# Gate and up with x stationary over 512 columns, twelve of 22 column blocks by seven half-products, down chunk by chunk

## The chip, the cores and the metric

The kernel runs on one core of a Trainium2 chip. The metric is the device time of one execution in microseconds, and the comparison is made on the median of several runs. A profile is one further execution, recorded by the hardware profiler; its span runs from the first to the last instruction, and its own device time is given beside it. Engines are named as the profile names them: PE (matrix unit; PEld is its weight load), DVE (vector), ACT (scalar), POOL (GpSimd) and SP (issues the DMAs).

## The reference

A trunk of two layers over x of 256 tokens by 1024 channels, float32. Each layer is a SwiGLU block, a mixer and a second SwiGLU block, every one behind an RMS norm and added to x:

```python
for layer in range(DEPTH):                     # DEPTH = 2, SEQ = 256, D_MODEL = 1024, D_FF = 2816
    x = x + 0.5 * _swiglu(_rmsnorm(x, ffn1_norm[layer]), gate, up, down)
    h = _rmsnorm(x, mix_norm[layer])
    x = x + (_even_mixer(h, ...) if layer % 2 == 0 else _pool_mixer(h, ...))
    x = x + 0.5 * _swiglu(_rmsnorm(x, ffn2_norm[layer]), gate, up, down)

def _swiglu(h, w_gate, w_up, w_down):
    return (jax.nn.silu(h @ w_gate) * (h @ w_up)) @ w_down
```

So there are four SwiGLU blocks, each with two products of 256x1024 by 1024x2816 and one of 256x2816 by 2816x1024. The even mixer has an input projection of 2560 columns, a spatial gate, attention over eight heads with a mask, and an output projection. The odd mixer multiplies four channel groups by 256x256 matrices and takes centred averages over the tokens.

## The kernel before

**Arithmetic.** Every large product is made in three passes over float32r operands: each operand a is split into a high part (a rounded by ACT when it writes float32r) and a low part (a minus the high part, on DVE), and high·high, high·low and low·high are accumulated in PSUM. `mm3` (L283) has the weights stationary, 128 by 128, and x moving, 256 tokens wide. `mm3x` (L289) has 128 tokens of x stationary and the weights moving; the even mixer's `natural` (L356) uses it over 512 columns.

**Weights.** All weights lie in DRAM as chunks of 16 blocks of 128 by 128 (1 MB), in the order of use: for a SwiGLU block 22 chunks of gate and up, one for each block of 128 columns of the hidden width, then 11 of down. `Weights` (L46) streams them: `load` (L63) issues one DMA of 1 MB into one of three `raw` tiles, `split_hi` (L79) makes `wh` by an ACT copy of 512 columns, `split_lo` (L89) makes `wl` by a DVE subtraction of 512 columns. Sixteen pairs of split tiles let the split run up to 15 steps of four blocks ahead of PE. `take` (L124) hands the next blocks to PE; at every fourth block `boundary` (L118) runs the small tasks that the code has put at that step with `at`, and then `pump` (L102) one or two splits. The order of each engine's queue is the order in which this code emits its instructions.

**A SwiGLU block** (`ffn`, L296). For each of 22 column blocks, gate and up are accumulated over the eight slices of the 1024 channels into two PSUM banks, hidden columns on the partitions and tokens along the row. `finish` (L302) puts three tasks at later steps: DVE multiplies by the row of norm factors and ACT takes the silu; DVE multiplies by up and ACT writes `yh`; DVE writes `yl`. All of y, 22 blocks high and low, is kept. After the last column block, down runs output block by output block (eight of them, 22 blocks of y each), and DVE scales the result by half the norm factor and adds it to X (L347, L348). `Norm` (L220) holds the next norm: x times gain, split high and low (L228, L231), the squares and their sum (L240, L242), and from it the factors: `columns` (L248) sums over partitions on PE, raises to the power −1/2 on POOL (L271) and refines on DVE; `rows` (L257) spreads them along the tokens by another PE product.

**Even mixer** (`even_mixer`, L366): `natural` for keys, queries, gate values and attention values, `prepare` (L419) for the norm and the rotary turn of queries and keys, `spatial`, `pair` for two heads, then the output projection into four banks and the update of X.

**Odd mixer** (`odd_mixer`, L602): four groups with x stationary, with `columns` emitted after the second of them; ACT and DVE copy the four banks scaled by the norm factors (L618, L619), then eight pairs of products with the averaging matrices (L626, L627) and the update of X (L628).

**Start.** x comes in four DMAs of 256 KB, the first chunk of weights in four DMAs between them (L173, L174). The first block's last products of each bank are held back until all of x is split.

Of the kernel before, what the change touches and what calls it, by code (L numbers as in the profile page):

```python
# [14 lines left out]
P = 128  # L15
# [15 lines left out]
PC = CT // STEP  # L31
RAW = 3
NB = 4

WARM = 20
KM = 5
EXTRA_AT = 2 * 33 + 33 + 14 + 1

# [6 lines left out]

class Weights:  # L46

    def __init__(self, nc, pools, src, extra, extra_at):
        self.nc = nc
        self.raw_pool, self.w_pool = pools
        self.src = src
        self.n = src.shape[0]
        self.extra, self.extra_at = extra, extra_at
        self.raw, self.parts = {}, {}
        self.dma = self.hi = self.lo = self.pos = 0
        self.tasks = {}  # L60
        self.paused = False

    def load(self, cuts=(0, CT)):  # L63

        c = self.dma
        if c >= self.n:
            return
        t = self.raw_pool.tile([P, CT * P], F32, name="raw")
        if c == self.extra_at:
            self.extra_at = None  # L70
            self.nc.sync.dma_start(t, self.extra)
            self.extra = t
            return
        for i, j in zip(cuts, cuts[1:]):
            self.nc.sync.dma_start(t[:, i * P:j * P], self.src[c, :, i * P:j * P])
        self.raw[c] = t
        self.dma += 1

    def split_hi(self, cuts=1):  # L79
        c, q = divmod(self.hi, PC)  # L80
        h = self.w_pool.tile([P, STEP * P], F32R, name="wh")
        self.parts[self.hi] = h, self.w_pool.tile([P, STEP * P], F32R, name="wl")
        raw = self.raw[c][:, q * STEP * P:(q + 1) * STEP * P]
        w = STEP * P // cuts
        for i in range(cuts):
            self.nc.scalar.activation(h[:, i * w:(i + 1) * w], raw[:, i * w:(i + 1) * w], AF.Copy)  # L86
        self.hi += 1

    def split_lo(self, cuts=1):  # L89
        c, q = divmod(self.lo, PC)  # L90
        h, l = self.parts[self.lo]
        raw = self.raw[c][:, q * STEP * P:(q + 1) * STEP * P]
        w = STEP * P // cuts
        for i in range(cuts):
            s = slice(i * w, (i + 1) * w)
            self.nc.vector.tensor_sub(l[:, s], raw[:, s], h[:, s].bitcast(F32))  # L96
        self.lo += 1
        if q == PC - 1:
            del self.raw[c]
            self.load()  # L100

    def pump(self, n):  # L102

        limit = min(self.pos // STEP + NB * PC - 1, self.n * PC)
        for _ in range(n):
            if self.hi < limit and self.hi // PC in self.raw:
                self.split_hi()
            if self.lo < min(self.hi, limit - 1) or self.lo < self.hi == self.n * PC:
                self.split_lo()

    @property
    def step(self):
        return self.pos // STEP
# [4 lines left out]
    def boundary(self):  # L118
        for f in self.tasks.pop(self.step, []):
            f()  # L120
        if not self.paused:
            self.pump(2 if self.step % 2 and self.step > 12 else 1)

    def take(self, n=1):  # L124

        if self.pos % STEP == 0:
            self.boundary()
        c, o = divmod(self.pos, STEP)
        assert o + n <= STEP
        while self.lo * STEP < self.pos + n:  # L130
            if self.hi == self.lo:
                self.split_hi()
            self.split_lo()
        self.pos += n
        wh, wl = self.parts.pop(c) if o + n == STEP else self.parts[c]
        return wh[:, o * P:(o + n) * P], wl[:, o * P:(o + n) * P]
# [3 lines left out]
def tile_encoder(ctx: ExitStack, tc: tile.TileContext, x, w, vecs, qk_gain, w_sp, b_sp, rope, mask, pool_op, eye, out):  # L140
# [3 lines left out]
    raw_pool = ctx.enter_context(tc.tile_pool(name="raw_pool", bufs=RAW))  # L144
    w_pool = ctx.enter_context(tc.tile_pool(name="w_pool", bufs=NB * PC))
    act = ctx.enter_context(tc.tile_pool(name="act", bufs=1))
    tmp = ctx.enter_context(tc.tile_pool(name="tmp", bufs=2))
    tiny = ctx.enter_context(tc.tile_pool(name="tiny", bufs=4))
    t2k = ctx.enter_context(tc.tile_pool(name="t2k", bufs=8))
# [4 lines left out]
    W = Weights(nc, (raw_pool, w_pool), w, pool_op, EXTRA_AT)  # L154

# [6 lines left out]
    def f32(ap):  # L162
        return ap.bitcast(F32)
# [4 lines left out]
    nc.sync.dma_start(vec, vecs)  # L168
    t0 = raw_pool.tile([P, CT * P], F32, name="raw")
    W.raw[0] = t0  # L170
    W.dma = 1
    for i in range(4):
        nc.sync.dma_start(X[:, 2 * i:2 * i + 2], x[:, 2 * i:2 * i + 2])  # L173
        nc.sync.dma_start(t0[:, i * 512:(i + 1) * 512], w[0, :, i * 512:(i + 1) * 512])  # L174
    W.load((0, 8, 16))
    W.load()
# [3 lines left out]
    gain = cst.tile([P, 2, HD], F32, name="gain")  # L180
    wsp = cst.tile([P, GROUPS, P], F32, name="wsp")
    bsp = cst.tile([P, GROUPS, P], F32, name="bsp")
    nc.sync.dma_start(ident, eye)

    def mixer_loads():
        nc.sync.dma_start(maskn, mask)
# [567 lines left out]
```

## Time and profile before

| | us |
|---|---|
| median of 3 runs | 892.8 |
| lowest and highest of them | 889.04, 893.38 |
| the profiled execution's own time | 890.89 |
| its span | 889.1 |

The profiled execution lies inside the runs shown. Its matmul records tell the stages: the first SwiGLU block's first matmul starts at 6.93 us, the even mixer at about 201.1, the second block at 300.57, the third at 491.52, the odd mixer at about 682.4, the fourth block at 693.91; the last matmul ends at 885.1, and the last store is issued at 886.05.

How to read the profile: the busy time of an engine is the time in which an instruction of it is recorded. Matmuls are pipelined, so one matmul's recorded duration (0.28 us for 256 columns) is longer than the step from its start to that of the next. The stage view gives, for a stretch of the span, the busy time and the number of instructions of each engine, the granted clock of PE as a share of full speed, the mean busy share of the 16 DMA engines and the GB/s moved. The chain of waits follows the end of the span back to what released each step. In the groups by line the columns are the line, engine and operation, output and inputs with their shape, the count, the busy time and the mean duration of one in ns, and the idle time ahead of them with what ended it.

### The profile page before, as it was taken

To read this page: it belongs to the slowest core of one execution; us is meant where nothing else is said; L and a number is where in the kernel's file an instruction comes from. 1 tells how busy PE (TensorE), PEld (TensorE's weight loads), DVE (VectorE), ACT (ScalarE), POOL (GpSimd) and SP (SyncE) were. 2 spreads that over 40 slices of the span, in tenths; PEclk is the share of its full clock that TensorE was granted. 3 is DMA by queue.
4 is the path that set the end of the run, shared out by engine and by line. 5 is a ranking of instruction groups with operands and counts; after the bars stand their busy time and mean duration, and the time that the engine had idled before them with its cause. 6 is when DMAs were issued, how large, how long until landed. Compare 5 with 4: busy or idle time off the path is not lost.

```text
span 889.1 us, 17465 instructions
## 1 busy us (share of the span) xinstructions
PE 879.4 (99%) x7088; PEld 864.3 (97%) x7088; DVE 594.1 (67%) x1147; ACT 497.0 (56%) x951; POOL 43.2 (5%) x44
## 2 busy tenths in 40 slices
PE   8999999999999999999999999999999999999998
PEld 7999999998788999999999999999999999999998
DVE  5678765667887776666566666666565976666551
ACT  6557654555667665555454555555444755555430
POOL 3000000003500300000000000000000200000000
PEclk9999999999999999999999999999999999999999
DMA  7568555454452365555445555555454565555430
GB/s 256 185 231 322 193 190 186 167 176 183 142 190 92 124 219 184 190 191 189 171 155 198 189 191 190 177 175 178 183 185 148 190 209 178 184 189 190 155 113 18
DMA packets 24704, 159.48 MB, mean 179 GB/s; under 512 B 2864, under 2 KB 4272, under 8 KB 5936
## 3 DMA queue, kind: packets, MB, share of 16 engines
q1 hardware_dynamic: 24624, 158.38, 50.9%
q8 instruction: 55, 0.90, 0.4%
q14 instruction: 25, 0.20, 0.1%
HBM read 157.32 MB, written 1.05 MB: 178 GB/s over the span
## 4 chain that ended last, share of the span: by engine, by line
PE 95%; DVE 2%; POOL 1%; DMA 1%; issue 1%; ACT 0%; SPq 0%; ACTq 0%; DVEq 0%
PE bank L285 30%; PE bank L287 30%; PE bank L286 30%; PE bank L291 1%; PE bank L292 1%; PE bank L293 1%; POOL rs_y L271 1%; DMA raw<-w_in 1%; DVE wl L96 1%; PE bank L533 1%; PE bank L502 0%; PE bank L525 0%; PE bank L626 0%; PE bank L252 0%; DVE t2k L453 0%
## 5 line engine op out<-in xcount | busy, mean ns | idle before, releaser
L86 ACT ACTIVATE wh<-raw 128x512 fp32r<-128x512 f32 (+1 forms) x589 | 355.5, 625 | 223.6 <-PE bank L286 204.6
L96 DVE TENSOR_TENSOR wl<-raw,wh 128x512 fp32r<-128x512 f32 (+1 forms) x589 | 395.9, 695 | 119.3 <-ACT wh L86 106.8
L285 PE MATMUL bank<-xh,wh 128*128 128x256 f32 x1440 | 408.6, 284 | 1.1 <-ACT xh L228 1.1
L287 PE MATMUL bank<-xh,wl 128*128 128x256 f32 x1440 | 408.1, 283 | 0.3 <-DVE wl L96 0.3
L286 PE MATMUL bank<-xl,wh 128*128 128x256 f32 x1440 | 407.7, 283 | 0.1
L285 PEld LDWEIGHTS bank<-xh,wh 128*128 128x128 f32 x1440 | 276.7, 192 | 1.3 <-ACT xh L228 1.3
L287 PEld LDWEIGHTS bank<-xh,wl 128*128 128x128 f32 x1440 | 276.5, 192 | 0.9 <-DVE wl L96 0.7
L286 PEld LDWEIGHTS bank<-xl,wh 128*128 128x128 f32 x1440 | 276.6, 192 | 0.4 <-DVE xl L231 0.3
L285 PE MATMUL bank<-yh,wh 128*128 128x256 f32 x768 | 218.1, 284 | 0.0
L287 PE MATMUL bank<-yh,wl 128*128 128x256 f32 x768 | 217.3, 283 | 0.0
L286 PE MATMUL bank<-yl,wh 128*128 128x256 f32 x704 | 199.2, 283 | 0.0
L285 PEld LDWEIGHTS bank<-yh,wh 128*128 128x128 f32 x768 | 147.3, 192 | 1.4 <-issue 1.0
L287 PEld LDWEIGHTS bank<-yh,wl 128*128 128x128 f32 x768 | 147.4, 192 | 0.0
L286 PEld LDWEIGHTS bank<-yl,wh 128*128 128x128 f32 x704 | 135.2, 192 | 0.0
L347 DVE TENSOR_TENSOR o<-bank,half 128x256 f32<-128x256 f32 x32 | 13.6, 425 | 87.7 <-PE bank L287 87.7
L228 ACT ACTIVATE xh<-X,vec 128x256 fp32r<-128x256 f32 x48 | 23.7, 506 | 75.4 <-DVE X L348 66.9
L312 DVE TENSOR_TENSOR y<-bank,t 128x256 f32<-128x256 f32 x88 | 37.3, 424 | 19.3 <-PE bank L287 18.3
L307 DVE TENSOR_TENSOR t<-bank,row 128x256 f32<-128x256 f32 x88 | 37.2, 423 | 13.8 <-PE bank L287 13.3
L308 ACT ACTIVATE t<-t 128x256 f32<-128x256 f32 x88 | 36.8, 418 | 14.5 <-DVE t L307 14.0
L313 ACT ACTIVATE yh<-y 128x256 fp32r<-128x256 f32 x88 | 36.8, 418 | 11.1 <-DVE y L312 10.0
L231 DVE SCALAR_TENSOR_TENSOR xl<-X,vec,xh 128x256 fp32r<-128x256 f32 x48 | 24.8, 525 | 21.5 <-ACT xh L228 21.4
L316 DVE TENSOR_TENSOR yl<-y,yh 128x256 fp32r<-128x256 f32 x88 | 36.9, 419 | 0.0
(92 smaller groups left out, 414.7 us busy)
## 6 DMA issues: line engine op xcount, KB each, us to landing
raw<-w_in SPq DMA_DIRECT2D x145, 1024.0 KB, 5.0
X<-x_in SPq DMA_DIRECT2D x4, 256.0 KB, 5.5
raw<-w_in SPq DMA_DIRECT2D x4, 256.0 KB, 6.6
raw<-w_in SPq DMA_DIRECT2D x2, 512.0 KB, 7.7
raw<-pool_in SPq DMA_DIRECT2D x1, 1024.0 KB, 6.0
out_dram<-X SPq DMA_DIRECT2D x8, 128.0 KB, 2.0
maskn<-mask_in SPq DMA_DIRECT2D x1, 256.0 KB, 5.2
wsp<-w_sp_in SPq DMA_DIRECT2D x1, 256.0 KB, 6.9
```

The costliest lines, as they stand in the source:

```text
L86: self.nc.scalar.activation(h[:, i * w:(i + 1) * w], raw[:, i * w:(i + 1) * w], AF.Copy)
L96: self.nc.vector.tensor_sub(l[:, s], raw[:, s], h[:, s].bitcast(F32))
L228: nc.scalar.activation(self.h[:, k], X[:, k], AF.Copy, scale=vec[:, self.g + k:self.g + k + 1])
L231: nc.vector.scalar_tensor_tensor(self.l[:, k], X[:, k], vec[:, self.g + k:self.g + k + 1], f32(self.h[:, k]), op0=OP.mult, op1=OP.subtract)
L285: nc.tensor.matmul(ps, lhsT=wh, rhs=xh, start=first, stop=False)
L286: nc.tensor.matmul(ps, lhsT=wh, rhs=xl, start=False, stop=False)
L287: nc.tensor.matmul(ps, lhsT=wl, rhs=xh, start=False, stop=last)
L307: nc.vector.tensor_mul(t, pg[:, :S], n.row)
L308: nc.scalar.activation(t, t, AF.Silu)
L312: nc.vector.tensor_mul(y, pu[:, :S], m["t"])
L313: nc.scalar.activation(yh[:, f], y, AF.Copy)
L316: nc.vector.tensor_sub(yl[:, f], m["y"], f32(yh[:, f]))
```

## The change

**Gate and up.** x becomes the stationary operand (128 tokens by 128 channels), and 512 columns of weights move: for an H part two column blocks, gate and up of both side by side, accumulated over the eight slices of the channels, for the two token halves in one bank each (`plain_chunk`). For an S part four column blocks, and the two by two block product (token halves by channel halves against channel halves by gate and up) is made by seven half-products instead of eight (`seven`): four sums of quarters of x (`combine`) are made once for each block, and sums of weights are made on DVE in place in the raw tiles (`Weights.sum`), split high and low like weights. A block's plan is "HHSHSHSH": five H parts of two column blocks and three S parts of four, 22 in all. Results have the tokens on the partitions; the norm factor is then a scale for each partition, and y is turned by PE transposes (`turned`) and split into a buffer for two parts (`yb`).

**Down** runs part by part: after each part PE takes the down products of the part before it, and all eight output blocks are accumulated in four banks throughout the block. The last two parts' down products end the block, pair of output blocks by pair.

**Weights.** Six raw tiles and four pairs of split tiles, all of a whole unit of 2048 columns; one ACT copy and one DVE subtraction split a whole unit. An S part takes four loads of 1 MB (2 KB rows), an H part two units of two DMAs each, down units one DMA for each output block (128 or 256 KB).

**Order.** The instructions' order is no longer tied to steps: `Order` keeps a clock for each engine, adds a constant price for each instruction emitted, and after every three matmuls emits on each other engine what is ready by these clocks, first from a list of small tasks and then from the stream of weights. PE's order is written in the code; `need` moves PE's clock forward until a task is done.

**Norms and mixers.** x times gain is kept (`xg`), pairs of slices are split at once, squares are summed on DVE instead of POOL. The mixers' tasks stay at their steps; `columns` of the odd mixer moves from after the second to after the fourth group, and its second stage updates X by pairs.

The diff, cut to its core:

```diff
-RAW = 3
-NB = 4
+UNIT = CT * P
+RAW = 6
+SPLIT = 4
+PLAN = "HHSHSHSH"
...
+class Order:
...
+    def step(self, e):
+        now = self.clock[e]
+        for i, t in enumerate(self.late[e]):
+            r = t.ready()
+            if r is not None and r <= now:
+                del self.late[e][i]
+                self.emit(t, r)
+                return
+        if self.stream[e]:
+            r = self.stream[e][0].ready()
+            if r is not None and r <= now:
+                self.emit(self.stream[e].popleft(), r)
+                return
+        self.clock[e] = now + 0.05
...
+            elif key == "V":
+                o.clock[key] += 0.16 + n / 960
+            elif key == "A":
+                o.clock[key] += 0.21 + n / 1230
...
+    def high(self, u, src, view):
+        def fn():
+            u.slot = self.split.get()
+            u.h, u.l = u.slot[1]
+            self.A.activation(view(u.h), view.raw(src.raw[1]), AF.Copy)
+        u.hi = self.add("A", fn, src.value, can=self.split.can)
+
+    def low(self, u, src, view, last):
+        def fn():
+            self.V.tensor_sub(view(u.l), view.raw(src.raw[1]), view(u.h).bitcast(F32))
+            if last:
+                self.raw.put(src.raw, self.o.clock["V"])
...
+    def ffn_stream(c0, first):
...
+            if kind == "H":
+                u["rows"] = [plain(gate_and_up(c0, f0, half), ROWS) if half or j or not first else Unit()
+                             for half in range(2)]
+                if j + 1 < len(PLAN):
+                    u["down"] = [b() for b in before]
+            else:
+                b11, b12 = gate_up(c0, f0, 0, 0), gate_up(c0, f0, 0, 1)
+                b21, b22 = gate_up(c0, f0, 1, 0), gate_up(c0, f0, 1, 1)
+                W.high(b11, b11, ROWS)
+                W.low(b11, b11, ROWS, False)
+                W.sum(b11, b12, (b11.hi, b11.ok))
+                W.high(b21, b21, ROWS)
+                W.low(b21, b21, ROWS, False)
+                t1 = u["t1"] = derived(b11)
+                W.low(t1, b11, ROWS, False)
+                W.sum(b11, b22, (t1.hi, t1.ok))
+                t2 = u["t2"] = derived(b11)
+                W.sum(b12, b22, ())
+                W.low(t2, b11, ROWS, False)
+                W.high(b22, b22, ROWS)
+                W.low(b22, b22, ROWS, True)
+                W.sum(b11, b21, (t2.hi, t2.ok), last=(b21,))
+                t3 = u["t3"] = derived(b12)
+                W.low(t3, b12, ROWS, True)
+                down = [before[0]()]
+                t4 = u["t4"] = derived(b11)
+                W.low(t4, b11, ROWS, True)
+                u["down"] = down + [b() for b in before[1:]]
...
+        def plain_chunk(u, buf):
+            ps = [ring_get() for _ in range(NT)]
+            for k in range(KD):
+                b = u["rows"][k // 4]
+                need(n.ok[k // 2], "x")
+                need(b.pieces[k] if hasattr(b, "pieces") and k < 4 else b.ok, "weights")
+                for t in range(NT):
+                    mm3x(ps[t][1], n.h[:, k, tok[t]], n.l[:, k, tok[t]], *rows(b, k % 4), k == 0, k == KD - 1)
...
+        def seven(u, buf):
...
+            product(pa, x_part(0, 0), u["b11"], True)
+            base, got1 = keep(pa)
+            product(pc, combo(0), u["t1"], True)
+            q5, got5 = keep(pc)
+            product(pb, x_part(1, 0), u["b21"], True)
+            g0, a0 = act(lambda: base[0], 0, add(base, pb, got1))
+            product(pa, combo(1), u["t2"], False, True)
+            u2, got2 = keep(pa)
+            product(pc, combo(3), u["b22"], False, True)
+            c12 = add(u2, pc, got2)
+            made = [whole(buf, g0, 0, gated(g0, lambda: u2[0], 0, 1, a0, c12))]
+            product(pa, combo(2), u["t3"], False, True)
+            c22 = add(q5, pa, got5, False)
+            downs(0)
+            product(pa, x_part(1, 1), u["t4"], False, True)
+            g1, a1 = act(lambda: pa[1], 1, free=lambda: pa)
+            made.append(whole(buf, g1, 1, gated(g1, lambda: q5[0], 1, 1, a1, c22)))
+            downs(1)
...
-            if g == 1:
+            if g == 3:
                 n.columns()
...
-    n = ffn(n, 1, first=True)
-    rope_tables()
+    n = first_pieces(units[0][0]["rows"][0])
+    n = ffn(n, units[0], 1, soon=[lambda: task("V", rope_tables, task("Q", mixer_loads))])
```

More of the change, by code (lines that the diff above doesn't have):

```diff
@@ L43 @@
 V_N = 60
-class Weights:
[L52 to L59, printed above, removed]
-        self.tasks = {}
[L61 to L113, printed above, removed]
@@ new lines, in down_blocks, with plain @@
+    def down_blocks(c0, f0, n, d0, dn):
+        parts = []
+        for d in range(dn):
+            s = (d0 + d) * KF + f0
+            done = 0
+            while done < n:
+                c, b = divmod(s + done, CT)
+                m = min(n - done, CT - b)
+                o = (d * n + done) * P
+                parts.append((lambda t, o=o, m=m: t[:, o:o + m * P], w[c0 + KF + c, :, b * P:(b + m) * P]))
+                done += m
+        return W.load(parts)
+    def plain(u, view=PLAIN):
+        W.high(u, u, view)
+        return W.low(u, u, view, True)
@@ L192, in tile_encoder, with first_pieces, load, high @@
-    W.at(40, mixer_loads)
+    units = [ffn_stream(0, True), chunk_stream(33, 14), ffn_stream(47, False), ffn_stream(80, False),
+             chunk_stream(113, 1), ffn_stream(114, False)]
+    def first_pieces(u):
+        u.raw, u.pieces = W.raw.get(), []
+        rows = u.raw[1].rearrange("p (g f k n) -> p g f k n", g=2, f=2, k=4)
+        def load(k):
+            if k == 0:
+                Q.dma_start(vec, vecs)
+            Q.dma_start(X[:, 2 * k:2 * k + 2], x[:, 2 * k:2 * k + 2])
+            for f in range(2):
+                src = w[f, :, :1024].rearrange("p (g k n) -> p g k n", g=2, k=4)
+                Q.dma_start(rows[:, :, f, k], src[:, :, k])
+        def high(k):
+            if k == 0:
+                u.slot = W.split.get()
+                u.h, u.l = u.slot[1]
+            A.activation(ROWS(u.h)[:, :, k], ROWS.raw(u.raw[1])[:, :, k], AF.Copy)
+        def low(k):
+            V.tensor_sub(ROWS(u.l)[:, :, k], ROWS.raw(u.raw[1])[:, :, k], f32(ROWS(u.h)[:, :, k]))
+            if k == 3:
+                W.raw.put(u.raw, O.clock["V"])
+        n = Norm(0)
+        for k in range(4):
+            a = task("Q", lambda: load(k))
+            O.emit_now(a)
+            n.pair(k, a, square=False)
+            u.pieces.append(task("V", lambda k=k: low(k), task("A", lambda k=k: high(k), a)))
+        for k in range(4):
+            n.square(k, u.pieces[k])
+        u.ok = u.pieces[-1]
+        O.emit_now(task("Q", lambda: Q.dma_start(ident, eye)))
+        return n
@@ L349, in ffn @@
             if m:
-                m.add(d)
+                m.pair(i, t)
             if store:
-                nc.sync.dma_start(out[:, d], X[:, d])
+                stored.append(task("Q", lambda: Q.dma_start(out[:, p], X[:, p]), t))
+        n0 = CT // older[2]
+        for i in range(5):
+            if i < 4:
+                d = 2 * i
+                down(older, f[-1][d // n0], d, 2, d // n0 * n0)
+            if i:
+                down(prev, f[-1][-1], 2 * i - 2, 2, last=finish)
+        for t in stored:
+            need(t)
```

765 lines of the change are left out of this document (532 added, 233 removed).

## The prediction

> **What bounds the kernel now.** I read the page's busy times first, then its slices and its chain of waits, then the stages.
>
> ```profile
> span 889.1 us, 17465 instructions
> PE 879.4 (99%) x7088; PEld 864.3 (97%) x7088; DVE 594.1 (67%) x1147; ACT 497.0 (56%) x951; POOL 43.2 (5%) x44
> PEclk9999999999999999999999999999999999999999
> PE 95%; DVE 2%; POOL 1%; DMA 1%; issue 1%; ACT 0%; SPq 0%; ACTq 0%; DVEq 0%
> ```
>
> PE is busy 99% of the span at full granted clock, and 95% of the chain that ended last lies on it. A busy PE can still hide pipelining, so the pace must come from a stage. The stage view (columns: stretch and its length; busy time and instruction count of PE, PEld, DVE, ACT, POOL; clock; DMA share; GB/s):
>
> ```profile
> 6.93:201.10 194.17, 192.64 (x1592) 191.58 (x1592) 132.57 (x250) 112.53 (x219) 7.29 (x8) 1.00 0.61 214
> 201.10:300.57 99.47, 97.79 (x620) 84.32 (x619) 77.13 (x189) 64.35 (x139) 22.66 (x15) 1.00 0.41 143
> 300.57:491.52 190.95, 190.95 (x1594) 190.95 (x1593) 130.00 (x237) 109.30 (x203) 5.12 (x6) 1.00 0.53 186
> 682.42:693.91 11.49, 11.49 (x87) 11.07 (x86) 7.89 (x22) 5.99 (x16) 2.49 (x4) 1.00 0.13 52
> 2.00:12.00 10.00, 8.29 (x43) 7.70 (x44) 3.78 (x9) 5.32 (x13) 0.00 (x0) 1.00 0.90 286
> 16.00:24.00 8.00, 8.00 (x68) 7.95 (x68) 4.98 (x7) 5.61 (x12) 5.71 (x7) 1.00 0.69 247
> ```
>
> The third row is one whole SwiGLU block (the second of four; the row ahead of all is the first, with the start in it): 1056 matmuls for gate and up, 528 for down, all 256 columns wide, and 8 records of statistics. No PE gap is left; DVE works 130 of 191 us. So a block costs what PE's instruction stream costs, until DVE comes near it. The second row is the even mixer, the fourth the odd one, and the last two are stretches near the start.
>
> **The change, part by part.** *PE stream.* The price of 512 columns is shown where the even mixer's first projection runs: 21 consecutive matmuls, first and last here. The transposes and the statistics come from the chain of waits.
>
> ```profile
> 201.25 0.40 PE L291 MATMUL bank<-wh,xh 128*128 128x512 f32 x1
> 205.81 0.39 PE L293 MATMUL bank<-wh,xl 128*128 128x512 f32 x1
> 269.64 0.44 PE bank L525 x4
> 498.89 0.34 PE bank L252 x4
> 502.20 0.45 PE bank L261 x4
> ```
>
> 20 steps in 4.56 us are 0.228 us each. A 256-column one costs (190.95 − 0.79) / 1584 = 0.120, so two cost 0.240: one wide matmul saves 0.012 on its pair. Per block the new plan HHSHSHSH has five H parts of 48 wide matmuls (8 slices of the contraction, 2 token halves, 3 passes) and three S parts of 84 (7 products, 4 slices, 3 passes; eight would be 96): 492 × 0.228 = 112.2 us for 1056 × 0.120 = 126.7, that is **−14.5**. Down keeps its 528 of 256 columns. New on PE are 44 transposes (4 for each H, 8 for each S) at 0.11 = **+4.8**; statistics go from 0.34 + 0.45 to 8 records, 0.68: **−0.1**. Net −9.8 per block, **−39 over four**.
>
> *DVE and ACT.* These must not become the limit. Rows by form, and one DVE step of the chain:
>
> ```profile
> L96 DVE TENSOR_TENSOR wl<-raw,wh 128x512 fp32r<-128x512 f32 x587 | 395.1, 696 | 119.3 <-ACT wh L86 106.8
> L96 DVE TENSOR_TENSOR wl<-raw,wh 128x256 fp32r<-128x256 f32 x2 | 0.8, 420 | 0.0
> L439 DVE TENSOR_TENSOR t2k<-t2k,tab 128x512 f32<-128x512 f32 x4 | 2.7, 678 | 0.0
> L86 ACT ACTIVATE wh<-raw 128x512 fp32r<-128x512 f32 x587 | 354.8, 626 | 223.5 <-PE bank L286 204.6 <-DMA raw<-w_in 9.6 <-PE bank L293 4.6
> L86 ACT ACTIVATE wh<-raw 128x256 fp32r<-128x256 f32 x2 | 0.7, 408 | 0.1
> 221.03 0.60 DVE wl L96
> ```
>
> Splits now take 2048 columns at once, a size the trace does not show. From 420 and 696 ns the slope is 1.08 ns a column, so 2.36 us; from the 0.60 us at which queued 512-column steps follow each other it is 2.26 at that slope, and 2.14 at the 1.0 that 678 against 420 gives. I take **2.2** (queued, which is how DVE will run) and keep 2.14 to 2.36. ACT: 626 + 1536 × 0.85 = 1.93 at most; I take 1.9. The rearranged views keep runs of 128 columns; L439, whose view has runs of 64, costs no more than a flat one, so I add nothing. Per block DVE does 42 low halves (10 for H, 21 for S, 11 for down) and 12 weight sums: 54 × 2.2 = 119 us; epilogues at 0.33 and 0.60 (0.09 under the time of one alone) are 3 × 4.2 + 5 × 1.3 = 19, the four combinations of x 8 × 0.60 = 4.8, norm and statistics 8: **151 of about 181 us, 83%**, for 130 of 191. ACT: 42 × 1.9 + 31 = 111, 61%.
>
> Within an S part it is not enough: 7 low halves, 4 sums, one down unit (12 × 2.2) and 4.2 of epilogue are 30.6 us of DVE beside 84 × 0.228 + 48 × 0.120 + 0.9 = 25.8 of PE. The missing 4.8 must have been done ahead, in the H part before, where DVE has 10 us for 23 us of PE (with two down units). Four split buffers allow three units ahead of the one in use. Following slots and order through one S (D the unit in use at its start, then b11, t1, b21, t2, b22, t3), t1 is ready before the start, t2 at 5.3 for 8.2, b22 at 7.6 for 10.9, t3 at 12.9 for 13.6: no wait, with 0.7 us to spare.
>
> The first S of a block is worse: after H, H and one down unit, with the combinations in between. There DVE has about 30 us of work for the 31 us until t1 is needed, and t3 comes about as it is needed: I put **0.5 us for each of the last three blocks, 1.5 in all**. In the first block DVE starts late (below) and has the rope tables too: t1 ready near 45 us, needed at 45.5; then two sums and a low half (6.6) make t2 late by 1, and b22, sum and t3 (6.6 and 1.2 of epilogue, for 5.5 of PE) by 2 more: **+3**.
>
> *Start.* From the timeline of the first 16 us:
>
> ```profile
> 1.18 0.42 SPq L173 DMA_DIRECT2D X<-x_in  x1
> 4.49 1.37 SPq L174 DMA_DIRECT2D raw<-w_in  x1
> 6.93 0.41 PE L285 MATMUL bank<-xh,wh 128*128 128x256 f32 x1
> 8.72 0.63 ACT L86 ACTIVATE wh<-raw 128x512 fp32r<-128x512 f32 x1 [1.85 <-DMA raw<-w_in]
> 10.67 0.63 ACT L86 ACTIVATE wh<-raw 128x512 fp32r<-128x512 f32 x1 [0.15 <-DMA raw<-w_in]
> 13.27 0.63 ACT L86 ACTIVATE wh<-raw 128x512 fp32r<-128x512 f32 x1 [0.25 <-DMA raw<-w_in]
> ```
>
> Pieces of x and weights land every 2 us, the third megabyte's first half by 13.3. The new first half-unit is again four pieces, and is through PE near 15. The second is one load of 1 MB, landing near 14, then 1.9 on ACT behind x's work and 2.2 on DVE as wholes, not in 0.6 steps: usable at 18.5 to 20.5, a wait of 3.5 to 5.5. Before, PE lost 194.17 − 190.95 = 3.2 us in the first block, part of which (2) stays and is not counted again: **+5**.
>
> *Odd mixer.* The statistics move from after the second group to after the fourth.
>
> ```profile
> 685.91 0.16 DVE L254 TENSOR_SCALAR v<-bank 128x2 f32<-128x2 f32 x1 [0.94 <-PE bank L252]
> 686.21 0.70 POOL L271 TENSOR_TENSOR rs_y<-v,mhalf 128x2 f32<-128x2 f32 x1 [186.01 <-DVE v L254]
> 687.33 0.16 DVE L278 SCALAR_TENSOR_TENSOR rs_r<-rs_a,rs_y 128x2 f32<-128x2 f32 x1
> 687.59 1.77 ACT L618 ACTIVATE yh<-bank,rs_r 128x256 f32<-128x256 f32 x4 [3.17 <-DVE rs_r L278]
> ```
>
> From 685.91 to the start of the first scaled copy is 1.7 us and 0.44 for the copy itself, until now beside the last two groups' matmuls. Now nothing covers it; groups three and four may also wait for x, whose chain queues behind splits of 2.2: **+3**, between 2 and 5.
>
> *Even mixer.* The same matmuls; DVE has 77 of 99 us, and a prepared step can queue behind a 2.2 us split instead of a 0.7 one: **+1**, from −2 (the 1.7 us that PE idled is gone) to +6.
>
> *DMA.* Same bytes. The down loads shrink to 128 or 256 KB with rows of 1 or 2 KB. The stage rows bound it: with 2 KB rows (2.00:12.00) a full share moves 286 / 0.90 = 318 GB/s, with 8 KB ones 358. The block's 186 GB/s at 0.53 become about 0.62: hidden. SP issues some 102 loads a block at about 0.47 us (eight begin from 1.18 to 4.49, quoted below), 50 of 181 us. S holds four of six raw buffers, but two come free by 10 us into it and the next H needs its second unit at 16.
>
> *Tail.* One 0.44 us DVE step before the last store goes: **−0.4**.
>
> **Sum.** −39 + 5 + 3 + 1.5 + 3 + 1 − 0.4 = −26. The profiled execution took 890.9 us (span 889.1), so **865 us**; that run lies inside the 889.0 to 893.4 of the runs shown, 2 below their median, and I do not correct for it.
>
> [...] The rows above show a queued DVE step beginning 0.60 after one that lasts 0.69. [...]
>
> [...]
>
> **Rivals.**
>
> 1. *DVE steps do not overlap when they are long* (2.36 each). An S then needs 28.3 + 4.9 = 33.2 for 25.8, nearly 3 us more than I counted, and 9 of 12 find 0.7 to spare: about 1 to 2 us for each S, +12 to +24: 877 to 889, say **880**. For it: the 696 rows. Against it: the 0.60.
> 2. *Nothing new waits*: start, first S and mixers as before: 890.9 − 39 − 0.4 = **851**. For it: DVE at 83%. Against: the uncovered statistics.
> 3. *Slower: DVE takes over.* If the order written out does not let DVE work ahead in H (a split slot or raw buffer freed late, an ACT copy queued behind a wait), each S runs at DVE's pace, 30.6 + 1.5 of handovers for 25.8: 12 × 6.3 = 76, so 865 + 76 − 4 = **937**. It turns slower than before once an S loses over 2.2 us beyond my count. For it: 30.6 against 25.8. Against it: the slots followed above, and that the constants by which the new order is made (0.69 and 0.63 us for 512 columns) are those of the rows L96 and L86.
> 4. *Small loads do not overlap*, each at the 2.0 us of the page's 128 KB store: 70 down loads × 2.0 + 12 of 1 MB × 5.0 + 20 of 512 KB × 3.5 = 270 us a block for 181, **1220**:
>
> ```profile
> raw<-w_in SPq DMA_DIRECT2D x145, 1024.0 KB, 5.0
> out_dram<-X SPq DMA_DIRECT2D x8, 128.0 KB, 2.0
> ```
>
> Against it: at the start eight loads of 256 KB, begun from 1.18 to 4.49, had landed before the row at 13.27, which waits for the ninth: 12 us, where one after another at 2.0 or more they would take over 16.
>
> **Chances.** Forecast (855 to 872) 0.56; first rival 0.19; second 0.15; third 0.08; fourth 0.02. Leaving out the last two and little of the second, the range is **849 to 886**. A measurement of this kernel tells about 0.5% (4.5 us, so 888 to 897 counts as the same): faster 0.87, same 0.05, slower 0.08.
>
> **What would show it.** Steps of 0.228 on the gate and up lines; queued 2048-column DVE steps at 2.2; PE gaps of 3 to 5 us near 15 us and of 2 to 3 in the odd mixer; no PE gap over 1 us in S parts after the first block; a block of about 181 us. I am wrong if PE waits for the low halves of t1 to t4 in every S, or if x or a PSUM bank holds PE between parts.

## The result, and the profile after

The changed kernel took **868.9 us** (median of 4 runs, 868.74 to 869.1) where the kernel before took 891.95 beside it (889.04 to 893.38): a ratio of 0.9746, interval 0.972 to 0.9772. The profiled execution took 868.89 us, its span is 867.1. Span against span the change gave 22.0 us; the prediction had put it at 26.

The page of the changed kernel: span, busy times, granted clock, the chain, one kind of load.

```profile
span 867.1 us, 12558 instructions
PE 845.1 (97%) x5016; PEld 740.3 (85%) x5016; DVE 706.5 (81%) x637; ACT 514.0 (59%) x524; POOL 24.6 (3%) x23
PEclk9999999999999999999999999999999999999999
PE 85%; DVE 7%; ACT 3%; issue 2%; DMA 2%; SPq 0%; POOL 0%; DVEq 0%; ACTq 0%; POOLq 0%
raw<-w_in SPq DMA_DIRECT2D x192, 128.0 KB, 4.8
```

PE still bounds the kernel, but no longer alone: its part of the chain fell from 95% to 85%, and DVE's rose from 2% to 7%. Nearly all instructions now carry one line number, that of the helper which issues them, so groups are told apart by their tiles. The slices show the clock as 9 everywhere, because a slice of 22 us hides what a finer view shows below.

The stages of the changed kernel, cut where those of before were (block one, even mixer, blocks two and three, odd mixer, block four), then three short stretches. Columns: stretch and length; busy time and count of PE, PEld, DVE, ACT, POOL; clock; DMA share; GB/s.

```profile
6.92:200.52 193.60, 185.99 (x1073) 160.74 (x1073) 161.56 (x134) 118.26 (x111) 2.65 (x1) 0.98 0.67 228
200.52:298.82 98.30, 97.02 (x622) 83.69 (x621) 75.17 (x136) 63.48 (x104) 16.81 (x12) 1.00 0.46 150
298.82:480.61 181.79, 181.04 (x1075) 159.55 (x1073) 153.99 (x118) 110.38 (x102) 2.65 (x1) 1.00 0.58 191
480.61:662.29 181.68, 180.93 (x1075) 159.50 (x1073) 154.28 (x116) 108.36 (x100) 0.70 (x1) 1.00 0.59 197
662.29:680.11 17.82, 14.15 (x91) 12.91 (x89) 12.49 (x20) 12.14 (x21) 0.70 (x1) 0.90 0.35 119
680.11:863.07 182.96, 181.51 (x1075) 159.51 (x1073) 147.08 (x115) 97.64 (x88) 0.70 (x1) 1.00 0.43 141
17.70:24.52 6.82, 5.20 (x11) 3.74 (x12) 5.91 (x9) 3.82 (x2) 2.65 (x1) 0.50 0.83 271
673.05:676.47 3.42, 3.28 (x10) 2.82 (x11) 1.92 (x5) 2.98 (x5) 0.00 (x0) 0.50 0.02 7
100.69:134.76 34.07, 34.07 (x178) 28.97 (x176) 30.50 (x20) 21.82 (x18) 0.00 (x0) 1.00 0.80 275
```

Two stages of before had no row yet, blocks three and four:

```profile
491.52:682.42 190.90, 190.90 (x1594) 190.90 (x1593) 126.27 (x233) 104.88 (x194) 0.70 (x1) 1.00 0.52 182
693.91:885.10 191.19, 191.19 (x1595) 190.99 (x1593) 118.18 (x215) 96.18 (x176) 4.54 (x6) 1.00 0.48 165
```

| stage | before, us | after, us | change | predicted |
|---|---|---|---|---|
| block one, start included | 194.17 | 193.60 | −0.6 | −9.8 + 5 + 3 = −1.8 |
| even mixer | 99.47 | 98.30 | −1.2 | +1 |
| block two | 190.95 | 181.79 | −9.2 | −9.8 + 0.5 = −9.3 |
| block three | 190.90 | 181.68 | −9.2 | −9.3 |
| odd mixer | 11.49 | 17.82 | **+6.3** | +3 |
| block four | 191.19 | 182.96 | −8.2 | −9.3 |
| last matmul to the end | 4.0 | 4.0 | 0.0 | −0.4 |

Blocks two and three came out as counted. What is missing lies in the odd mixer (3.3), in the first and fourth blocks (about 1 each) and in the tail (0.4); the even mixer gave 2.2 back, which is luck, since its +1 was put at anything from −2 to +6. The last stretch, 100.69 to 134.76, is the second S part of block one from its second product on, with the gate and up products of the H part behind it: PE busy through all 34.07 us, DVE through 30.50 of them. So a later S part does run without a gap. The two rows with a clock of 0.50 show something the prediction did not have.

Where PE waits. A wait is given here as the time by which a matmul begins later than one step (0.228 or 0.120 us) after the one before it; the bracket in the timeline counts from the modelled end of that one and is smaller. The timeline of the changed kernel at the start (start, duration, engine, operation), then in the first S part of block two, then in the odd mixer:

```profile
15.72 1.91 ACT L173 ACTIVATE wh<-raw 128x2048 fp32r<-128x2048 f32 x1 [0.21 <-DMA raw<-w_in]
16.58 1.02 PE L173 MATMUL bank<-ones,acc 128*128 128x1 f32 x8 [1.20 <-DVE acc L173]
17.68 0.80 PE L173 MATMUL bank<-wh,xh 128*128 128x512 f32 x1
17.75 2.29 DVE L173 TENSOR_TENSOR wl<-raw,wh 128x2048 fp32r<-128x2048 f32 x1
20.10 0.80 PE L173 MATMUL bank<-wl,xh 128*128 128x512 f32 x1 [1.62 <-DVE wl L173]
...
328.35 4.49 DVE L173 TENSOR_TENSOR raw<-raw,raw 128x2048 f32<-128x2048 f32 x2
333.52 4.49 DVE L173 TENSOR_TENSOR wl<-raw,wh 128x2048 fp32r<-128x2048 f32 x2 [0.68 <-ACT wh L173]
338.53 2.28 DVE L173 TENSOR_TENSOR raw<-raw,raw 128x2048 f32<-128x2048 f32 x1
340.74 2.28 DVE L173 TENSOR_TENSOR wl<-raw,wh 128x2048 fp32r<-128x2048 f32 x1
341.78 0.63 PE L173 MATMUL bank<-wh,combos 128*128 128x512 f32 x2
343.07 0.50 PE L173 MATMUL bank<-wl,combos 128*128 128x512 f32 x1 [0.66 <-DVE wl L173]
...
669.99 0.95 PE L173 MATMUL bank<-ones,acc 128*128 128x1 f32 x8
671.28 0.70 POOL L173 TENSOR_TENSOR rs_y<-v,mhalf 128x2 f32<-128x2 f32 x1 [179.85 <-DVE v L173]
672.41 0.16 DVE L173 SCALAR_TENSOR_TENSOR rs_r<-rs_a,rs_y 128x2 f32<-128x2 f32 x1
672.66 1.57 ACT L173 ACTIVATE yb<-bank,rs_r 128x256 f32<-128x256 f32 x4 [4.75 <-DVE rs_r L173]
673.19 1.22 PE L173 MATMUL bank<-combos,yb 128*128 128x256 f32 x2 [2.25 <-ACT yb L173]
```

At the start the second half-unit lands at 15.7, ACT rounds it as a whole until 17.6, DVE takes its remainder until 20.0, and PE stands at 17.9 to 20.1. In block two the sum that starts at 338.53 and the low half of t3 (340.74 to 343.0) come in a row; the two matmuls of 341.78 leave PE free at 342.24, it goes on at 343.07: a wait of 0.83. In the odd mixer the chain from the statistics to the scaled copy stands alone on the path, 2.25 us of idle PE. All three places are those that the prediction named. At the first, PE ran at half clock (0.50) from 17.70 to 24.52, that is from before the wait of 2.2 us; behind the last, from 673.05 to 676.47.

### The profile page after: what moved, and what is told of

It reads as the page before. It is cut to its first block, busy times and chain, and to the rows that moved or that the text cites. A ratio compares the mean times of both kernels' runs of the same rounds, so it can differ in the third digit from the quotient of the medians.

```text
span 867.1 us, 12558 instructions
## 1 busy us (share of the span) xinstructions
PE 845.1 (97%) x5016; PEld 740.3 (85%) x5016; DVE 706.5 (81%) x637; ACT 514.0 (59%) x524; POOL 24.6 (3%) x23
## 3 DMA queue, kind: packets, MB, share of 16 engines
HBM read 157.32 MB, written 1.05 MB: 183 GB/s over the span
## 4 chain that ended last, share of the span: by engine, by line
PE 85%; DVE 7%; ACT 3%; issue 2%; DMA 2%; SPq 0%; POOL 0%; DVEq 0%; ACTq 0%; POOLq 0%
PE bank L173 85%; DVE wl L173 4%; DMA raw<-w_in 1%; ACT wh L173 1%; DVE raw L173 1%; DVE t2k L173 1%; DMA X<-x_in 1%; ACT xg L173 0%; DVE acc L173 0%; ACT t2k L173 0%; SPq L173 0%; DVE X L173 0%; DVE yb L173 0%; DVE xl L173 0%; ACT L173 0%
## 5 line engine op out<-in xcount | busy, mean ns | idle before, releaser
L173 DVE TENSOR_TENSOR wl<-raw,wh 128x2048 fp32r<-128x2048 f32 (+1 forms) x186 | 416.2, 2254 | 72.4 <-ACT wh L173 69.2
L173 ACT ACTIVATE wh<-raw 128x2048 fp32r<-128x2048 f32 (+1 forms) x186 | 349.5, 1886 | 173.9 <-PE bank L173 102.2
L173 PE MATMUL bank<-yb,wh 128*128 128x256 f32 x1536 | 275.0, 281 | 0.0
L173 PEld LDWEIGHTS bank<-yb,wh 128*128 128x128 f32 x1536 | 235.9, 188 | 3.8 <-issue 1.0
L173 PE MATMUL bank<-wh,xh 128*128 128x512 f32 (+1 forms) x544 | 214.7, 395 | 1.1 <-ACT xh L173 0.7
L173 PE MATMUL bank<-yb,wl 128*128 128x256 f32 x768 | 214.9, 280 | 0.3
L173 PE MATMUL bank<-wl,xh 128*128 128x512 f32 (+1 forms) x544 | 211.9, 390 | 2.5 <-DVE wl L173 2.5
L173 PE MATMUL bank<-wh,xl 128*128 128x512 f32 (+1 forms) x544 | 211.5, 389 | 1.4 <-DVE xl L173 1.4
L173 PEld LDWEIGHTS bank<-yb,wl 128*128 128x128 f32 x768 | 144.3, 188 | 1.2 <-DVE wl L173 1.2
L173 PE MATMUL bank<-wh,combos 128*128 128x512 f32 x384 | 125.5, 396 | 0.0
```

The costliest lines, as they stand in the source:

```text
L173: return f(*args, **kw)
```

## The experiments

Every kernel below is the changed kernel with one edit, or with the edits named. Times are medians with their extremes, each ratio is to the kernel before, measured in the same set; the changed kernel's own are 868.9 and 0.9746 (0.972 to 0.9772).

### h11: the half-products taken out

```diff
-PLAN = "HHSHSHSH"
+PLAN = "HHHHHHHHHHH"
...
-                    n.combine()
+                    if "S" in PLAN:
+                        n.combine()
```

> Every SwiGLU block is eleven parts of the plain kind (PLAN = eleven H), so no half-products and no sums of weights or of x; the result is the same function. Theory (the half-products are worth their count): per block 36 wide matmuls more at 0.227 us, +8.2; the waits in front of low halves in the first S part go, -0.8 to -1.1 in three blocks and -4 in the first; transposes and down are as they are. 868.9 + 32.7 - 7 = 895 (890 to 898), about the kernel before. Rival (x stationary over 512 columns and the chunked down carry the gain, the half-products give theirs back in waits on DVE): 866 to 875.

901.41 us (899.21 to 902.06), ratio 1.0113 (1.0091 to 1.0136). The first of its groups by shape (768 wide matmuls of each kind where the changed kernel has 528 and 192), and three stretches of its stages:

```profile
L173 PE MATMUL bank<-wh,xh 128*128 128x512 f32 x768 | 302.3, 394 | 0.0
```

```profile
199.00:204.00 5.00, 5.00 (x45) 5.00 (x44) 1.98 (x3) 2.61 (x6) 0.00 (x0) 1.00 0.50 203
486.50:491.50 5.00, 5.00 (x30) 5.00 (x31) 1.38 (x2) 2.06 (x4) 0.00 (x0) 0.66 0.70 210
678.50:683.50 5.00, 5.00 (x32) 5.00 (x31) 1.38 (x2) 2.06 (x4) 0.00 (x0) 0.66 0.59 202
```

All gate and up work is 512 columns wide here and DVE is at ease (busy 55% of the span), yet the kernel is 1.1% slower than before. So the width alone doesn't pay for the new order's transposes and waits; the gain is in the three S parts. Their count is 36 wide matmuls less per block, 36 × 0.228 × 4 = 32.8 us, and the two kernels differ by 32.5. The time lies 3 above the range that I gave it. The expectation missed this: the plan drops the S parts' waits but has others of its own, 2.09 us of PE gap three times, at 195.99, 484.15 and 675.59, where the last down products of a block wait for the remainder of y from DVE. The agreement with the count is to that extent lucky. The stages show what becomes of three gaps of one size: over the 5 us behind the second and the third the clock averages 0.66, behind the first it stays at 1.00.

### fill and fill2: idle matmuls against the half clock

```diff
+                if k == 4 and hasattr(u["rows"][0], "pieces"):
+                    for _ in range(FILL1):
+                        nc.tensor.matmul(accs[0][:, :S], lhsT=xh[:, 0, :P], rhs=xh[:, 0], start=True, stop=True)
...
             if g == 3:
                 n.columns()
+                spare = bank2()
+                for _ in range(FILL2):
+                    nc.tensor.matmul(spare[:, :S], lhsT=xh[:, 0, :P], rhs=xh[:, 0], start=True, stop=True)
```

> 36 matmuls of 256 columns into an unused bank stand ahead of the first part's second half, and 18 behind the odd mixer's statistics, where PE idles; no other instruction moves. Theory (the half clock of 18.0 to 24.9 us and of 673.4 to 676.8 comes from these idle stretches): the granted clock stays 1.0 throughout, the matmuls after the gaps step by 0.227 and not 0.427, -2.5 at the start and -1.8 in the odd mixer: 864.6 (863.5 to 866). Rival (the low clock has another cause, or the time there is DVE's and not PE's): 868 to 870.

fill (36 and 18 matmuls): 869.92 (868.44 to 871.05), ratio 0.9763 (0.9742 to 0.9784). The odd mixer kept its clock, but the start became worse. The start's timeline:

```profile
15.04 4.47 PE L784 MATMUL bank<-xh 128*128 128x256 f32 x36
19.36 0.95 PE L174 MATMUL bank<-ones,acc 128*128 128x1 f32 x8
20.17 0.48 PE L174 MATMUL bank<-wh,xh 128*128 128x512 f32 x1
22.80 0.80 PE L174 MATMUL bank<-wl,xh 128*128 128x512 f32 x1 [2.15 <-DVE wl L174]
```

The statistics' products, which stood at 16.58 before, now stand behind the filling in PE's queue. DVE's step that reads them is queued ahead of the low half that PE needs next, so the filling delayed the very thing it was to bridge. fill2 puts 10 idle matmuls ahead of the statistics' products and 18 behind the first matmul of the second half:

> As fill, with the start's filling put where PE idles without anything behind it that DVE waits for: 10 unused matmuls ahead of the statistics' products, 18 behind the first matmul of the second half-unit; 18 in the odd mixer as before. Theory (fill kept the odd mixer's clock and lost 2.5 us at the start because the statistics' products stood behind the filling, DVE's mean behind them, and the low half behind that): the low half is ready at 20.0 as in the changed kernel, the clock stays 1.0, and the start gains 2 to 2.7, the odd mixer 1.5: 868.9 - 4 = 865 (864 to 866). Rival (what follows the start is limited by DVE and the loads, so that PE only waits later): the odd mixer's part alone, 867 to 868.

fill2: 867.72 (867.03 to 867.96), ratio 0.9744 (0.973 to 0.9759). That is 1.2 us under the changed kernel, but the ratio is the same, so the times alone don't show a gain. By the stages of its profiled execution the odd mixer takes 16.30 us for 17.82, and block one 194.54 for 193.60, still with half clock from 19.46 to 22.88 (0.55 from 19.90 to 23.20): 1.5 from the odd mixer, nothing from the start, as the rival had it.

### quarters: the second half-unit in four pieces

```diff
+            def high(k=k):
...
+                self.A.activation(ROWS(u.h)[:, :, k], ROWS.raw(u.raw[1])[:, :, k], AF.Copy)
+            def low(k=k):
+                self.V.tensor_sub(ROWS(u.l)[:, :, k], ROWS.raw(u.raw[1])[:, :, k], ROWS(u.h)[:, :, k].bitcast(F32))
```

> The second half-unit of the first part is split by four ACT copies and four DVE subtractions of 512 columns and used piece by piece, its load as it is. Theory (PE's wait at 15 to 20 us is the 1.91 + 2.29 us of the whole-unit split behind a load that lands at 15.7): the first piece is usable near 17.0, the wait falls from 4.1 to about 1.8 us, and the idle stretch is too short for the clock to drop: -2.3 and up to -2.5 more, 864 to 866.7. It does not change the first S part's waits by more than 1. Rival (the load itself is the limit): 868 or more.

870.1 (869.14 to 870.43), ratio 0.9764 (0.9745 to 0.9783). The theory's gain did not come. The wait of 2.2 us at 17.9 went. Another of 2.26 came at 26.17, where PE has run ahead to the transposes whose input isn't there yet, and the first S part's first two waits grew from 1.20 and 1.08 to 1.44 and 1.33. The clock kept its full rate through the start, but halved from 29.57 to 32.99, behind that wait. The start is paced by loads (a DMA share of 1.05 from 24.50 to 29.50 here, 1.03 from 24.50 to 29.00 in the changed kernel) and by DVE; the wait removed in it came back further on.

### swap: the sum b11 + b21 moved behind t3's low half

```diff
-                W.sum(b11, b21, (t2.hi, t2.ok), last=(b21,))
                 t3 = u["t3"] = derived(b12)
                 W.low(t3, b12, ROWS, True)
+                W.sum(b11, b21, (t2.hi, t2.ok), last=(b21,))
```

> In each S part the third sum on the left operand (b11 += b21, which only the seventh product needs) moves from ahead of t3's low half to behind it on DVE. Theory (PE waits in the first S part because DVE's queue, not a buffer, is late; t3's low half stands behind that sum): the waits ahead of t3 go (0.83, 0.83, 0.89 and 1.5 us in the four blocks), nothing new, since 48 down products lie between t3 and t4: 868.9 - 4 = 865 (864 to 866.5). Rival (the wait only moves, to the down unit or to t4, whose split now starts 2.2 us later): 868 to 870.

878.41 (877.85 to 879.74), ratio 0.9863 (0.9839 to 0.9886), worse than both expectations. The wait for t3 is gone, and its timeline shows where it went:

```profile
347.24 0.48 PE L173 MATMUL bank<-yb,wh 128*128 128x256 f32 x2
350.02 0.39 PE L173 MATMUL bank<-yb,wl 128*128 128x256 f32 x1 [2.31 <-DVE wl L173]
```

```profile
350.00:354.50 4.50, 4.48 (x25) 4.48 (x26) 4.50 (x3) 1.18 (x1) 0.00 (x0) 0.62 0.93 298
738.30:741.70 3.40, 3.38 (x28) 3.38 (x29) 3.40 (x3) 1.25 (x1) 0.00 (x0) 1.00 0.95 199
```

The down unit behind t3 is now late, by 2.47 us instead of 0.25, in blocks two to four (2.08 in block one). In blocks one to three the gap is followed by a half-clock stretch, as the first stage row shows for block two (0.62 over 4.5 us); behind the gap of block four, which ends at 738.32, the clock stays at 1.00 (second row). DVE's sum of work is the same; only its order changed, and it cost 9.5 us. The order written out is the better of the two by far, and a gap above 2 us can cost more than its length: behind block two's, PE is busy for 4.48 of the 4.50 us at 0.62 of its clock, by estimate another 0.38 × 4.5 = 1.7 us.

### pause: no splits in the queues during the odd mixer's first part

```diff
-        if self.stream[e]:
+        if self.stream[e] and not self.paused:
```

> From the odd mixer's first matmul to its statistics, no weight split is put into the queues of DVE and ACT. Theory (two of the odd mixer's waits, 0.83 and 0.91 us on the low halves of x, are a 2.2 us split that DVE had begun): they shrink by 0.6 to 1.7 in all, the 2.4 us behind the statistics stays and the clock still drops; nothing is lost in the fourth block, whose second unit is needed 5 us after its start: 867.2 to 868.4. Rival (the chain add, gain, high, low is itself 3.5 us long, and the split hides behind it): 868.7 to 869.2.

868.96 (867.8 to 869.48), ratio 0.9758 (0.9743 to 0.9772). One of the mixer's two waits for x shrank from 0.91 to 0.38, and the total didn't move: the rival. Half a microsecond is less than these runs can tell; the 2.39 behind the statistics stayed.

### pool: three of the squares' additions on POOL

```diff
+                if self.g // KD in (2, 3, 5):
+                    self.summed = task("G", lambda: G.tensor_tensor(self.acc, self.acc, sq[0], op=OP.add), self.summed)
+                else:
```

> In the norms ahead of blocks two, three and four the three additions of squares go from DVE to POOL. Theory (PE's 0.83 to 0.9 and 0.25 us waits in the first S part of these blocks come from DVE's total work since the block began, not from the order of one part): 1.8 us less of DVE work takes them away, -1.1 in each of three blocks: 865.6 (865 to 866.5), if POOL's reads do not hold DVE up. Rival (POOL and DVE hold each other up, or ACT waits for the squares' buffers): 868 to 872.

871.48 (870.85 to 872.67), ratio 0.9785 (0.9769 to 0.9802). The waits for t3 stayed as they were (0.84, 0.90, 0.90), though in the stretch of block two that reaches from 13.1 to 48.2 us behind its start DVE is busy for 32.95 us here and for 34.25 in the changed kernel. So DVE's *total* work since the start of the block isn't what makes t3 late, and that theory fell. At the start of block four a wait of 0.82 grew to 1.73. Its timeline there:

```profile
683.12 1.51 POOL L173 TENSOR_TENSOR acc<-acc,sq 128x512 f32<-128x512 f32 x1 [9.53 <-ACT sq L173]
683.42 1.75 DVE L173 TENSOR_TENSOR xl<-xg,xh 128x512 fp32r<-128x512 f32 x1
685.23 0.50 PE L173 MATMUL bank<-wh,xl 128*128 128x512 f32 x1 [1.56 <-DVE xl L173]
...
685.88 0.68 DVE L173 TENSOR_TENSOR xl<-xg,xh 128x512 fp32r<-128x512 f32 x1
```

The low half of x takes 1.75 us beside the POOL addition and 0.68 alone, with the same shape and tiles: it ends 0.54 after POOL does. That is the rival, for DVE beside POOL; what holds DVE up, the rows don't show.

### load: one more DVE step in every S part

```diff
                 W.low(t1, b11, ROWS, False)
+                W.low(t1, b11, ROWS, False)
```

> Every S part gets one more DVE step of 2048 columns, 2.2 us: the low half of t1 is made twice. Theory (DVE has no room in a block's first S part and 3.5 us of idle time in each later S and H pair, as the changed kernel's window of 100.69 to 134.76 shows: 30.5 busy of 34.1): 2.2 to 3.9 in each of four blocks, the upper end where the longer wait lets the clock drop, and nothing from the other eight S parts: 878 to 885. Rival, as the prediction counted it (t3 has 0.7 us to spare in the later S parts): 1.5 more in each of eight, 890 to 897.

889.74 (888.24 to 891.13), ratio 0.9988 (0.9975 to 1.0001): twelve DVE steps, 26 us of its time, cost 21 us and the whole gain. That is next to the rival, the prediction's own count. One of the later S parts, by its timeline:

```profile
401.15 0.63 PE L173 MATMUL bank<-wh,combos 128*128 128x512 f32 x2
402.60 0.49 PE L173 MATMUL bank<-wl,combos 128*128 128x512 f32 x1 [0.82 <-DVE wl L173]
```

PE waits 0.99 here (402.60 − 401.15 − 2 × 0.23) and 0.25 once more behind it; seven of the eight later S parts do the same, the last waits 1.21. From 2.2 us added, 1.24 show, so about 1.0 was to spare where the prediction had counted 0.7. The first S parts lose more: 4.05 for t1 alone in block one. DVE is less than one step away from being the bound.

### early: the combinations of x ahead of the first H part

pool had ruled out the total. What remained was *when* DVE does its work. Two stretches of the changed kernel's second block, the first before the four combinations enter DVE's queue behind the first H part, the second from there through the first S part:

```profile
303.00:312.00 9.00, 9.00 (x45) 7.57 (x44) 6.81 (x12) 6.62 (x7) 2.65 (x1) 1.00 0.27 83
311.90:347.00 35.10, 34.35 (x181) 28.82 (x180) 34.25 (x29) 23.58 (x23) 0.00 (x0) 1.00 0.36 111
```

DVE idles for 2.2 of the first 9.0 us, and for 0.9 of the next 35.1. The edit, in blocks two to four:

```diff
+                if j == 0 and not soon:
+                    n.combine()
                 made = plain_chunk(u, buf)
                 if j == 0:
-                    n.combine()
+                    if soon:
+                        n.combine()
...
-                v = task("V", fn, *deps)
+                v = task("V", fn, *self.gained, *deps)
```

> In blocks two to four the combinations of x are put into the queues ahead of the first H part in place of behind it; block one is left as it was. In the changed kernel's second block DVE has idle pieces until 311 us and none from 311.9 to 347, and the first S part waits 0.83 for t3 and 0.25 for its down unit (0.89 in the third and fourth blocks); four sums and four low halves of 0.6 (4.8 us) lie in the busy stretch. Theory (the prediction's term 'the first S of a block is worse ... with the combinations in between', measured 1.1 where 0.5 was put): with the combinations in the idle pieces these waits go from blocks two to four, about 3.3 us: 865.6 (865 to 866.5) against 868.9. Rival: the combinations push the low halves of x or of the first units of the block back, and the wait reappears at the block's start or with t1: 867.5 to 870.

866.77 (866.27 to 869.09), ratio 0.9741 (0.972 to 0.9761), against 0.9746 for the change: a gain the times alone don't show. Its stages do:

```profile
299.20:480.27 181.07, 180.72 (x1075) 159.60 (x1074) 153.91 (x118) 110.60 (x102) 1.01 (x1) 1.00 0.58 192
480.27:661.37 181.10, 180.73 (x1075) 159.58 (x1074) 154.43 (x116) 109.05 (x100) 1.01 (x1) 1.00 0.59 198
```

Blocks two and three are 0.72 and 0.58 shorter, for 1.1 expected: the waits for t3 are gone in all three blocks, while those for the down unit grew from 0.25 to 0.5. Theory right, size half to two thirds. Block four is 0.7 shorter too, but in the profiled execution the odd mixer lost 0.9 (18.72 for 17.82), with the clock halved in it for 6.8 us instead of 3.4 (the mean granted clock of the execution is 0.991 for 0.994).

### early_fill, again and early_odd: the best version, and what the start's half clock costs

> The run before and the idle matmuls of the run called fill2 together (10 ahead of the statistics' products in the first part, 18 behind the first matmul of its second half, 18 behind the odd mixer's statistics; their sums are in a bank that is overwritten or unused). Theory: the two gains are in different stages and add: 868.9 - 3.3 - 1.2 = 864.4 (863.5 to 865.5). Rival: as in the run before, with the fill's 1.2 alone: 866.5 to 868.5.

early_fill: 864.79 (863.56 to 866.07), ratio 0.9715 (0.9695 to 0.9734). The gains add. The mean granted clock of its profiled execution was 1.0, where the changed kernel's was 0.994, but block one still had its first S part's waits of 1.2, 1.1 and 1.5. To tell the start's filling from the odd mixer's, early_odd leaves it out, and again is the changed kernel once more beside it:

> The changed kernel as it is, once more, beside the next run on the same chip, to see how much of a microsecond at the start and in the clock comes and goes by itself. So far its first block ended at 200.4 us, kernels with the same start ended it between there and 200.8. Theory (the half clock is part of this kernel, not of one execution): the granted clock halves again for two windows of 3.4 us near 18 to 25 us and for one or two behind the odd mixer's 2.4 us gap; 868 to 870. Rival: the drops are chance; no drop, or at another place, 865 to 867 in some of the five runs.

> The combinations early and 18 idle matmuls behind the odd mixer's statistics, but none at the start. Beside the run called early it tells what the odd mixer's filling is worth alone, and beside early_fill what the start's filling is worth. Theory: the odd mixer's filling keeps the clock and takes its gap, 2.3 us (odd mixer and block four took 200.8 in early and 198.4 in early_fill); the start's filling gives the other 1.1 (first block to 199.6 in place of 200.8): 865.5 (865 to 866.3). Rival: the start's filling gives nothing, as in fill2, where block one ended at 200.9: 864.4 to 865.

again: 869.61 (868.84 to 870.87), ratio 0.9777 (0.9763 to 0.979), with the clock halved at both places as before (its mean is 0.994 again): the drops belong to this kernel. Its ratio was 0.9746 in the first set and is 0.9777 in this one, so a microsecond can only be told within one set. early_odd: **864.82** (864.59 to 865.24), ratio 0.9718 (0.9705 to 0.9732), 4.8 us under the changed kernel in the same set, and no different from early_fill. The rival holds: the start's filling gives nothing. At the start PE's half clock costs nothing that can be measured: the first S part of block one waits 1.2, 1.1 and 1.5 for DVE's low halves with it and without it. Only in the odd mixer is it on the path. The odd mixer of early_odd by timeline and as a stage:

```profile
668.25 0.95 PE L174 MATMUL bank<-ones,acc 128*128 128x1 f32 x8
669.06 2.39 PE L669 MATMUL bank<-xh 128*128 128x256 f32 x18
671.44 5.66 PE L174 MATMUL bank<-combos,yb 128*128 128x256 f32 x32
```

```profile
660.55:676.86 16.31, 14.88 (x109) 13.69 (x107) 12.50 (x20) 11.36 (x20) 0.69 (x1) 1.00 0.41 130
```

The idle matmuls fill the same gap, 669.06 to 671.44, and shorten nothing in it; the stage still falls from 17.82 to 16.31 at a clock of 1.00 for 0.90. So 1.5 us of the odd mixer's +6.3 were the clock.

## Why the prediction was right, and where its terms were off

**PE stream: right.** Predicted −9.8 per block. Block two less its two waits is 181.79 − 0.83 − 0.25 = 180.7, which is 10.2 under 190.95; the matmuls step at 0.227 where 0.228 was taken.

**DVE's long step: right, and the first rival fell.** 2.2 us were taken, between 2.14 and 2.36. Two queued sums take 4.49, 2.29 and 2.20; the low half of 340.74 follows the sum of 338.53 by 2.21. The steps overlap by 0.09 as the short ones do, so the first rival (2.36 each, 880 us) is out. DVE's work per block was counted at 151 us and is 154.0.

**S parts: right for the later ones, too little for the first.** No wait in the later ones (the 34.07 us row), with about 1.0 to spare for 0.7. For the first ones 0.5 each was put in blocks two to four, and they wait 1.08, 1.08 and 1.14; block one waits 1.20, 1.08, 1.51 and 0.25, 4.0 for 3. The cause given, the combinations in between, is shown by early for t3, whose waits go with them; the down unit's grew. In blocks two and three the 0.6 too little here and the 0.4 by which the PE stream came out lower nearly cancel, which is luck.

**Start: right in kind.** A wait of 3.5 to 5.5 was predicted for the second half-unit. PE loses 1.4 ahead of the statistics' products and 2.2 and 0.4 behind them, 4.0. The load landed at 15.7 for 14. The whole block came out 1.2 above its prediction. The half clock there was not foreseen either, but costs nothing that the runs can tell.

**Odd mixer: the step that failed in size.** "+3, between 2 and 5" became +6.3. The uncovered chain is 2.39, against the 2.1 (1.7 and 0.44) of the working; the waits for x, for which the +3 left 0.9, are 0.83 and 0.91; and 1.5 is the half clock, which the prediction did not have at all. The statistics, for which it added nothing here, take eight records and 0.81 us (668.25 to 669.06 in early_odd), where before four took 0.36:

```profile
685.37 0.50 PE L252 MATMUL bank<-ones,acc 128*128 128x1 f32 x4
685.73 0.36 PE L291 MATMUL bank<-wh,xh 128*128 128x256 f32 x1
```

These are 6.1 of the 6.3; the other 0.2 isn't traced.

**Even mixer and tail.** The even mixer gained 1.2 where +1 was taken, within −2 to +6; its transposes still wait 1.27. The tail's −0.4 didn't come (4.0 for 4.0).

**DMA: right, and the other rivals fell.** A share of about 0.62 was estimated for a block, 0.58 is measured; the 128 KB loads take 4.8 us each and overlap (192 of them one after another would be 922 us, more than the span), so the fourth rival is out. "Nothing new waits" (851) and "DVE takes over" (937) are out too, though load shows how near the second is: 2.2 us more of DVE work in each S part took the whole gain.

## What to carry to other kernels

When a change trades matmuls for work on another engine, count that engine's work stretch by stretch and in queue order, not as a share of the whole: here 81% busy left about 1 us to spare in the S parts, and moving one 2.2 us step the wrong way cost 9.5 us. Look for idle pieces ahead of a tight stretch and move into them what is ready early, as early did. And price a new PE gap of 2 us and more with the slow clock that can follow it (1.5 us in the odd mixer here); where that is on the path, idle matmuls in the gap are cheap (18 of them brought that stage from 17.82 us to 16.3), provided they stand behind everything that others wait for.

## What the runs showed of the hardware

**The clock can halve behind a gap of about 2 us.** Gaps of 2.1 to 2.5 us, mostly with smaller ones or the statistics' one-column products close by, were followed by half clock for 3.4 us (row 673.05:676.47) or 6.8 (the odd mixer of early); the single wait of 1.5 at 61.3 was not (the clock is 1.00 from 61.00 to 68.00). At the start the clock had halved at 17.70 already, behind a wait of 1.4 and the statistics (row 17.70:24.52). Length alone doesn't decide: of three gaps of 2.09 us in h11 two dropped the clock (0.66 over the 5 us behind each, 1.00 behind the first), of four gaps in swap three did, and the one that didn't was 2.47 long (row 738.30:741.70). In the changed kernel the half-clock stretches last 6.82 and 3.42 us (6.827 and 3.413 in the trace's clock records), and their starts are 673.05 − 17.70 = 655.35 apart, 192 times 3.413. Why one gap drops the clock and another of its length doesn't, the runs don't show.

**A POOL addition stretched a DVE step.** A DVE step with two inputs that takes 0.68 us alone took 1.75 beside an addition on POOL of 1.51 (run pool), and PE waited 1.73 instead of 0.82 for it: an engine that is 3% busy in the changed kernel wasn't free to use.
